# Entering the second feed-forward block: the last head pair's 1/z and the sums of squares on VectorE, three output tiles interleaved, statistics one tile later

## The chip, the cores and the metric

The kernel runs on one core of one Trainium2 chip. The metric is the device time of one execution in microseconds (us). Before the change three runs took 2205.42, 2205.99 and 2206.07 us; the median is 2205.99 us. The profile is one execution, taken with the hardware profiler.

The engines are named as the profile names them: PE multiplies matrices (PEld is its weight load), DVE is VectorE, ACT is ScalarE, POOL is GpSimd and SP is SyncE. SP, ACT and POOL also issue DMA transfers. Each engine executes its own instructions in the order in which the program wrote them, and waits at an instruction until its inputs are there.

## The reference, cut to what matters

A decoder trunk of two layers over 1024 positions of 1024 features. Layer 0 mixes tokens with a short gated convolution, layer 1 with dilated attention (16 heads of 64). A SwiGLU feed-forward block follows each.

```python
for i in range(DEPTH):                       # DEPTH = 2
    h = rms_norm(x, mix_norm[i])
    if i % N_MIXERS == 0:
        x = x + short_conv_mixer(h, ...)
    else:
        x = x + dilated_attention_mixer(h, ..., rel_bias)
    h = rms_norm(x, ffn_norm[i])
    x = x + swiglu(h, ffn_w_gate[i], ffn_w_up[i], ffn_w_down[i])
return rms_norm(x, final_norm)

def rms_norm(x, g):
    return x * rsqrt(mean(x * x, axis=-1) + EPS) * g
```

Two parts of it matter here. The attention output of a head is a sum `o` over keys divided by a sum of weights `z`; the kernel computes `o` and `z` and then multiplies `o` by 1/z. It is followed by the output projection with `attn_w_out`, which is added to x. Then `rms_norm` needs, for every position, the sum of squares over all 1024 features of the new x, before the feed-forward block can use any of it.

## The kernel before

The residual stream is held transposed, as eight tiles `X[0..7]` of 128 features by 1024 positions. Everything is 32-bit; a product takes three matmuls, because both operands are split into a rounded high part and a low remainder. `split` (L128) makes the two parts: ACT copies the high part (L138), DVE subtracts it from the source (L139). Weights come as raw slabs by SP's DMAs (`load_raw`, L148) and are split in the order of the list `ops`; `ensure` (L159) writes the splits up to a given place of that list into the program, and `take` hands one out and ensures one more ahead.

Attention works through eight pairs of heads. `slot` writes the instructions of one head and fills them up with matmuls of an independent product (`dense`). `finish` (L1482) turns the sums of a pair into attention output. For pairs 0 to 6 it sends z to DRAM, reads it back as a 128x16 tile, takes the reciprocal there, and reads 1/z back, spread over the partitions. For the last pair the first half of the positions is done on DVE directly, in two pieces of 256 columns (L1516, then o times 1/z, L1510, then the split into `o_hi` and `o_lo`). The second half goes through DRAM on POOL's queue (L1503, L1505, reciprocal of a 128x8 tile at L1528, L1529, L1530), and what remains to be done with it, the function `rest`, is put into the list `last_part`.

The output projection is done in two groups of heads. The first five pairs are multiplied beneath the attention. The last three pairs (k = 5, 6, 7, where 7 is the last pair) are `group1` of `into_ffn(1, ...)`, which calls `by_columns` (L1168): the first half of the positions (column half 0) for all eight output tiles n, then the second half. In column half 0 the first `AO_WIDE` = 5 tiles are interleaved on PE: k = 5 of all five, k = 6 of all five, then k = 7 of all five. The other tiles follow one by one, nine matmuls each. After each tile come, in this order: `add_to_x` (DVE, L459), `added` (which ensures the coming weight slabs), `each` (which is `chained`) and `between`.

`chained` (L411) squares the new half tile on ACT (L420) and sums the squares. Tile 0 is squared into `acc`, tile 1 into a second sum. Tiles 2 to 5 are added by accumulating DMAs that POOL issues (L422), alternately to the two. Tiles 6 and 7 and the second sum are added by DVE (L423).

`between` sends the half tile to DRAM from ACT's queue (L1211). At tile 3 of column half 0 it asks for the first feed-forward slabs (L1214) and runs `rest`. At tile 7 it finishes the sum and loads ACT's table for the square root (L1222). In column half 1, after tile 0, it writes the statistics of the first half: four small matmuls that sum over the partitions (L438), a square root (L441), a reciprocal (L442), a diagonal tile (L447), and three sums of raw weights (`combos`, L186). After tile 1 a matmul spreads the result (L454) and ACT copies it to `rstd` (L455). From there tiles 1 to 7 each carry one or two steps of `first_half` (L1061: DVE normalises a half tile, L1056, ACT and DVE split it, L518 and L519) and of `gained` (L1073: ACT writes the other half of the tile, times its gain, over the first half; for n > 3 POOL adds two of these with an accumulating DMA, L1082).

The feed-forward block follows in the same instruction streams: after its first product `last_step` writes the last split of `first_half` and the last addition of a square, after its second product come the statistics of the second half (L438 again), and after its third product the spread and `second_half` (L1084).

The first layer uses the same `into_ffn` with i = 0 and four interleaved tiles.

Of the kernel before, what the change touches and what calls it, by code (L numbers as in the profile page):

```python
# [10 lines left out]
F32 = mybir.dt.float32  # L11
F32R = mybir.dt.float32r
AF = mybir.ActivationFunctionType
ALU = mybir.AluOpType
# [3 lines left out]
S = 1024  # L18
# [5 lines left out]
HALF = 512  # L24
NPAIR = H // 2
# [20 lines left out]
AO_WIDE = 5  # L46
# [48 lines left out]
def trunk(ctx: ExitStack, tc: tile.TileContext, x, gains_in, cwi, ck, cwo, wqkv, wo, relb,  # L95
          wg, wu, wd, oneh, ident, out):
    nc = tc.nc
# [3 lines left out]
    dram = ctx.enter_context(tc.tile_pool(name="dram", bufs=1, space=DRAM))  # L101
# [5 lines left out]
    scope = {}  # L107

    def half_page(name, dt=F32):
        return scope["pool"].tile([128, 512], dt, name=name, tag="half", bufs=scope["halves"])  # L110
# [259 lines left out]
    X = [None] * KT  # L370

    class Norm:
        def __init__(self, gi):
            self.g = gi
            self.h = {}
            self.acc = self.rstd = None
            self.put_off = None

        def flush(self):

# [30 lines left out]
        def chained(self, k, c0, c1):  # L411

            s = slice(c0, c1)
            if self.acc is None:
                self.acc, self.rstd = page("acc"), page("rstd")
            acc = self.acc[:, s]
            if k == 1:
                self.odd = half_page("acc2")
            to = half_page("sq") if k > 1 else self.odd if k else acc
            nc.scalar.activation(to, X[k][:, s], AF.Square)  # L420
            if 1 < k < 6:
                nc.gpsimd.dma_start(out=(acc, self.odd)[k % 2], in_=to, accum_op=ALU.add)  # L422
            add = lambda t: nc.vector.tensor_tensor(out=acc, in0=acc, in1=t, op=ALU.add)  # L423
            if k == KT - 1:
                self.flush()
                add(self.odd)
                self.odd = None
            if k > 5:
                self.put_off = lambda: add(to)
# [759 lines left out]
    def into_ffn(i, norm):  # L1189

        sw = Swiglu(i, norm)

        pre = []
        first_op = [k for k, f in ops].index(("m", (i, 0), 1))

        def step(k):
            next(pre[0], None)
            sw.gained(k)

        def group1(key, ks, acts):  # L1200
            def added(j, n):

                if j == 0 and n > 3:
                    if n + 2 < KT:
                        ensure(op_state[1] + 1)
                    ensure(first_op + n - 4)
                elif j and n < 2:
                    ensure(first_op + n + 4)

            def between(j, n):  # L1210
                nc.scalar.dma_start(spill[n][:, half(j)], X[n][:, half(j)])  # L1211
                if j == 0:
                    if n == 3:
                        load_raw(raw_base[i] + 3)  # L1214
                        if not i:
                            nc.scalar.activation(less, gains, AF.Copy, scale=-1.0)
                        if last_part:
                            last_part.pop()()
                    elif n == KT - 1:
                        norm.flush()  # L1220
                        if i:
                            nc.scalar.activation(scratch, eps, AF.Sqrt)  # L1222
                elif n == 0:
                    pre.append(norm.stats(0, HALF))
                    next(pre[0])
                    for m in (6, 7):
                        combos[i, 0](m)
                else:
                    if n == 1:
                        run(pre.pop())  # L1230
                        pre.append(sw.first_half())
                    for k in ((0,), (1,), (2, 3), (4,), (5,), (6,), (7,))[n - 1]:
                        step(k)

            by_columns((key, 1), ks, acts, HALVES, lambda n, c: norm.chained(n, *c), between,
                       AO_WIDE if key == "ao" else 4, added=added)

        def last_step():
            run(pre[0])
            norm.flush()  # L1240

        return sw, group1, norm.stats(HALF, S), last_step


# [9 lines left out]

    vdram = [dram.tile([S, 256], F32, name=f"vdram{g}") for g in range(NPAIR // 2)]

    zdram = [[dram.tile([2, S], F32, name=f"{x}dram{n}") for x in "zr"] for n in range(NPAIR)]

    def blk(j):
        return (j // 4) * HALF + (j % 4) * 8  # L1260
# [1 line left out]
    def attention(norm):  # L1262
# [11 lines left out]
        parts = {}  # L1274
# [207 lines left out]
        def finish(p):  # L1482

            o, z = OZ.pop(p)
            if p < NPAIR - 1:
                zd, rd = zdram[p]
                nc.sync.dma_start(zd, z[0:65:64])
                yield
                zc = scope["pool"].tile([128, 16], F32, name="zc", tag="zc", bufs=2)
                nc.sync.dma_start(zc, bass.AP(zd.tensor, zd.offset, [[16, 128], [1, 16]]))  # L1490
                yield
                nc.vector.reciprocal(zc, zc)
                nc.sync.dma_start(bass.AP(rd.tensor, rd.offset, [[16, 128], [1, 16]]), zc)
                yield
                nc.sync.dma_start(z, bass.AP(rd.tensor, rd.offset, [[S, 2], [0, 64], [1, S]]))
                yield
                put_off.append((p, o, z))
                return

            zd, rd = zdram[p]  # L1500
            wide = lambda t: bass.AP(t.tensor, t.offset, [[HALF, 2], [1, HALF]])
            thin = lambda t: bass.AP(t.tensor, t.offset, [[8, 128], [1, 8]])
            nc.gpsimd.dma_start(wide(zd), z[0:65:64, HALF:])  # L1503
            zc = scope["pool"].tile([128, 8], F32, name="zl", tag="zl", bufs=1)
            nc.gpsimd.dma_start(zc, thin(zd))  # L1505
            acts[p] = page("o_hi", F32R), page("o_lo", F32R)

            def scaled(c0, c1):
                q = slice(c0, c1)
                nc.vector.tensor_tensor(out=o[:, q], in0=o[:, q], in1=z[:, q], op=ALU.mult)  # L1510

            def parts(h):
                split(o[:, half(h)], [t[:, half(h)] for t in acts[p]])

            for c in (0, 256):
                nc.vector.reciprocal(z[:, c:c + 256], z[:, c:c + 256])  # L1516
                scaled(c, c + 256)
                if c:
                    parts(0)
                yield  # L1520

            def rest():
                scaled(HALF, S)
                parts(1)

            last_part.append(rest)
            yield
            nc.vector.reciprocal(zc, zc)  # L1528
            nc.gpsimd.dma_start(thin(rd), zc)  # L1529
            nc.gpsimd.dma_start(z[:, HALF:], bass.AP(rd.tensor, rd.offset, [[HALF, 2], [0, 64], [1, HALF]]))  # L1530
            yield

        def attended():

# [157 lines left out]
    nc.vector.memset(eps, EPS)  # L1692
    nc.vector.memset(zcol, 0.0)

    last_part = []
    with tc.tile_pool(name="first", bufs=1) as scope["pool"]:
        scope["halves"] = 20
        conv = Conv(Norm(0))
# [2 lines left out]
        norm = Norm(1)  # L1701
# [11 lines left out]
    with tc.tile_pool(name="third", bufs=1) as scope["pool"]:  # L1713
# [3 lines left out]
        norm = Norm(4)  # L1717
# [135 lines left out]
```

## Time and profile before

| | |
|---|---|
| runs | 2205.42, 2205.99, 2206.07 us |
| span of the profiled execution | 2203.1 us; its own time is the span and about 2.9 us around it, taken from the median of the runs |
| PE busy | 2138.2 us, 97% of the span |
| DVE busy | 1752.9 us, 80% |
| ACT busy | 1000.5 us, 45% |
| POOL busy | 170.7 us, 8% |
| mean granted PE clock | 0.989 |

How to read it: the page lists busy time by engine for the whole span. A PE that is 97% busy says little about one stage, so the stage of the change is read from timelines of single engines (start, duration, line, operation, and in brackets the idle time before it and what ended it), from groups of instructions within a window, and from windows with the granted clock. The stage lies between 1484 and 1555 us.

### The profile page before, as it was taken

The numbers are of one execution on the slowest core, as the hardware profiler recorded it, in microseconds if no ns is written. First come the engines' busy times: TensorE is split into PE (matmuls) and PEld (weight loads), VectorE is DVE, ScalarE is ACT, GpSimd is POOL, SyncE is SP. The second block draws the span as 40 slices with busy tenths as digits, with TensorE's granted clock in tenths as the row PEclk, the third lists the DMA queues.
The fourth block names the chain that finished last, engine by engine and source line by source line (L and its number), as shares of the span: only waits on it lengthen the run. The fifth ranks groups of instructions, "written<-read, shape, count | busy, mean of one in ns | idle before, by whom it ended". The sixth has DMA issues, their size and how long they took to land. (4 is left out here: it accounts for less than half of the span.)

```text
span 2203.1 us, 30573 instructions
## 1 busy us (share of the span) xinstructions
PE 2138.2 (97%) x11138; PEld 1825.5 (83%) x11138; DVE 1752.9 (80%) x3229; ACT 1000.5 (45%) x1812; POOL 170.7 (8%) x224
## 2 busy tenths in 40 slices
PE   7899999999999999999999999998999999999998
PEld 6788888778888878878999998886778888888887
DVE  7797758988888798865677777866888888889886
ACT  6433426434444444445455455534544444454435
POOL 0000001100101000010111111112000101000000
PEclk9999999999999999999999999998999999999999
DMA  4122543223323384323333333446223233366432
GB/s 155 55 86 71 210 153 87 96 91 100 116 96 120 117 281 144 119 68 131 91 91 92 94 97 90 152 154 170 77 77 102 105 105 111 96 226 204 158 91 77
DMA packets 135345, 261.89 MB, mean 119 GB/s; under 512 B 48328, under 2 KB 59608, under 8 KB 135194
## 3 DMA queue, kind: packets, MB, share of 16 engines
q1 hardware_dynamic: 75978, 184.80, 26.3%
q0 software_dynamic: 18048, 52.03, 7.0%
q10 hardware_dynamic: 41168, 23.10, 3.5%
q8 instruction: 88, 1.44, 0.3%
q14 instruction: 63, 0.52, 0.1%
HBM read 187.31 MB, written 66.27 MB: 115 GB/s over the span
## 5 line engine op out<-in xcount | busy, mean ns | idle before, releaser
L526 PE MATMUL bank<-b,w 128*128 128x512 f32 x1784 | 704.6, 395 | 25.6 <-DVE part L536 6.4
L528 PE MATMUL bank<-b,w 128*128 128x512 f32 x1784 | 700.4, 393 | 8.9 <-DVE w L139 8.9
L527 PE MATMUL bank<-b,w 128*128 128x512 f32 x1784 | 701.4, 393 | 0.0
L526 PEld LDWEIGHTS bank<-b,w 128*128 128x128 f32 x1784 | 338.6, 190 | 102.6 <-ACT part L532 7.4
L528 PEld LDWEIGHTS bank<-b,w 128*128 128x128 f32 x1784 | 338.7, 190 | 84.2 <-DVE w L139 13.1
L527 PEld LDWEIGHTS bank<-b,w 128*128 128x128 f32 x1784 | 338.7, 190 | 69.2 <-issue 0.7
L138 ACT ACTIVATE w<-combo 128x512 fp32r<-128x512 f32 (+2 forms) x464 | 234.5, 534 | 281.5 <-DVE combo L186 275.5
L139 DVE TENSOR_TENSOR w<-combo,w 128x512 fp32r<-128x512 f32 (+2 forms) x464 | 260.9, 576 | 57.5 <-ACT w L138 55.2
L532 ACT ACTIVATE part<-bank 128x512 f32<-128x512 f32 x168 | 99.5, 593 | 269.7 <-PE bank L528 258.6
L139 DVE TENSOR_TENSOR w<-raw,w 128x512 fp32r<-128x512 f32 (+2 forms) x316 | 169.4, 561 | 15.6 <-ACT w L138 14.1
L536 DVE TENSOR_TENSOR part<-part,bank 128x256 f32<-128x256 f32 (+1 forms) x348 | 159.1, 488 | 26.4 <-PE bank L528 14.2
L138 ACT ACTIVATE w<-raw 128x512 fp32r<-128x512 f32 (+2 forms) x316 | 150.7, 519 | 46.0 <-PE bank L528 11.2
L747 DVE TENSOR_TENSOR x<-x,bank 128x512 f32<-128x512 f32 x168 | 114.6, 682 | 30.7 <-PE bank L528 30.7
L347 PE MATMUL bank<-w_hi,w 128*128 128x512 f32 (+1 forms) x320 | 121.3, 379 | 4.4 <-ACT w L138 4.4
L349 PE MATMUL bank<-w_hi,w 128*128 128x512 f32 (+1 forms) x320 | 119.3, 373 | 0.9 <-DVE w L139 0.9
L348 PE MATMUL bank<-w_lo,w 128*128 128x512 f32 (+1 forms) x320 | 119.0, 372 | 0.0
L459 DVE TENSOR_TENSOR x<-x,bank 128x512 f32<-128x512 f32 (+1 forms) x104 | 66.1, 643 | 65.6 <-PE bank L349 57.3
L186 DVE TENSOR_TENSOR combo<-raw 128x512 f32<-128x512 f32 (+1 forms) x160 | 103.2, 645 | 4.0 <-DMA raw<-in_conv_w_in 4.0
L347 PE MATMUL bank<-h_hi,w_hi 128*128 128x512 f32 x256 | 104.6, 408 | 0.0
L349 PE MATMUL bank<-h_hi,w_lo 128*128 128x512 f32 x256 | 100.2, 391 | 0.7 <-DVE w_lo L139 0.7
L348 PE MATMUL bank<-h_lo,w_hi 128*128 128x512 f32 x256 | 99.9, 390 | 0.0
L1130 ACT ACTIVATE part<-part 128x512 f32<-128x512 f32 x66 | 39.7, 628 | 107.5 <-DVE part L536 107.5
(252 smaller groups left out, 3842.7 us busy)
## 6 DMA issues: line engine op xcount, KB each, us to landing
hin<-part SPq DMA_DIRECT2D x126, 256.0 KB
raw<-in_ffn_w_gate SPq DMA_DIRECT2D x44, 512.0 KB
raw<-in_ffn_w_up SPq DMA_DIRECT2D x44, 512.0 KB
part<-sum POOLq DMA_DIRECT2D x72, 256.0 KB, 2.7
raw<-in_ffn_w_down SPq DMA_DIRECT2D x48, 384.0 KB
x<-spill SPq DMA_DIRECT2D x24, 512.0 KB
raw<-in_attn_w_qkv SPq DMA_DIRECT2D x24, 512.0 KB
raw<-in_conv_w_in SPq DMA_DIRECT2D x21, 512.0 KB
```

The source lines that it names most:

```text
L138: nc.scalar.activation(hi, src, AF.Copy)
L139: eng.tensor_tensor(out=lo, in0=src, in1=hi, op=ALU.subtract)
L186: eng.tensor_tensor(out=c, in0=a, in1=b, op=op)
L347: nc.tensor.matmul(b, whi[:, a], ahi[:, s], start=first, stop=False)
L348: nc.tensor.matmul(b, whi[:, a], alo[:, s], start=False, stop=False)
L349: nc.tensor.matmul(b, wlo[:, a], ahi[:, s], start=False, stop=last)
L526: nc.tensor.matmul(b, hi[:, a], bhi, start=start and k == 0, stop=False, skip_group_check=True)
L527: nc.tensor.matmul(b, hi[:, a], blo, start=False, stop=False, skip_group_check=True)
L528: nc.tensor.matmul(b, lo[:, a], bhi, start=False, stop=k == n - 1, skip_group_check=True)
L532: nc.scalar.activation(t, b, AF.Copy)
L536: nc.vector.tensor_tensor(out=t, in0=t, in1=b, op=ALU.add)
L747: nc.vector.tensor_tensor(out=X[n][:, half(h)], in0=X[n][:, half(h)], in1=b, op=ALU.add)
```

## The change

For i = 1 only, unless said otherwise:

1. `finish` of the last pair takes all four pieces of 256 columns on DVE. The four small DMAs, the 128x8 reciprocal, `rest` and `last_part` are gone, and so are the DRAM tiles for that pair.
2. `chained` no longer uses accumulating DMAs or the second sum when `by_dma` is false (it stays true for i = 0). Every square of tiles 1 to 7 is added to `acc` by DVE, one tile later than it is made.
3. Three tiles instead of five are interleaved in column half 0. `ahead_ao` in the attention keeps the constant 5, so the splits of weight slabs 0 to 4 stay where they were; the slabs 5 and 6, which `by_columns` ensured ahead of its first products, are now ensured with tile 4.
4. The statistics of column half 0 are written after tile 1 of column half 1, not after tile 0; the spread and the steps of `first_half` and `gained` start a tile later, with two steps at tile 2 and two at tile 7.

```diff
@@ class Norm
             self.put_off = None
+            self.by_dma = True
@@ chained
             acc = self.acc[:, s]
+            if not self.by_dma and k:
+                to = half_page("sq")
+                nc.scalar.activation(to, X[k][:, s], AF.Square)
+                self.flush()
+                self.put_off = lambda: nc.vector.tensor_tensor(out=acc, in0=acc, in1=to, op=ALU.add)
+                return
             if k == 1:
                 self.odd = half_page("acc2")
@@ into_ffn
         sw = Swiglu(i, norm)
+        norm.by_dma = not i
+        begin = i
@@ between
                         if not i:
                             nc.scalar.activation(less, gains, AF.Copy, scale=-1.0)
-                        if last_part:
-                            last_part.pop()()
                     elif n == KT - 1:
                         norm.flush()
                         if i:
                             nc.scalar.activation(scratch, eps, AF.Sqrt)
-                elif n == 0:
+                elif n == begin:
                     pre.append(norm.stats(0, HALF))
                     next(pre[0])
                     for m in (6, 7):
                         combos[i, 0](m)
-                else:
-                    if n == 1:
+                elif n > begin:
+                    if n == begin + 1:
                         run(pre.pop())
                         pre.append(sw.first_half())
-                    for k in ((0,), (1,), (2, 3), (4,), (5,), (6,), (7,))[n - 1]:
+                    plan = ((0, 1), (2,), (3,), (4,), (5,), (6, 7)) if i else ((0,), (1,), (2, 3), (4,), (5,), (6,), (7,))
+                    for k in plan[n - begin - 1]:
                         step(k)
 
             by_columns((key, 1), ks, acts, HALVES, lambda n, c: norm.chained(n, *c), between,
-                       AO_WIDE if key == "ao" else 4, added=added)
+                       3 if key == "ao" else 4, added=added)
@@ attention
-    zdram = [[dram.tile([2, S], F32, name=f"{x}dram{n}") for x in "zr"] for n in range(NPAIR)]
+    zdram = [[dram.tile([2, S], F32, name=f"{x}dram{n}") for x in "zr"] for n in range(NPAIR - 1)]
@@ finish
-            zd, rd = zdram[p]
-            wide = lambda t: bass.AP(t.tensor, t.offset, [[HALF, 2], [1, HALF]])
-            thin = lambda t: bass.AP(t.tensor, t.offset, [[8, 128], [1, 8]])
-            nc.gpsimd.dma_start(wide(zd), z[0:65:64, HALF:])
-            zc = scope["pool"].tile([128, 8], F32, name="zl", tag="zl", bufs=1)
-            nc.gpsimd.dma_start(zc, thin(zd))
             acts[p] = page("o_hi", F32R), page("o_lo", F32R)
@@ finish
-            for c in (0, 256):
+            for c in range(0, S, 256):
                 nc.vector.reciprocal(z[:, c:c + 256], z[:, c:c + 256])
                 scaled(c, c + 256)
-                if c:
-                    parts(0)
+                if c % HALF:
+                    parts(c // HALF)
                 yield
-
-            def rest():
-                scaled(HALF, S)
-                parts(1)
-
-            last_part.append(rest)
-            yield
-            nc.vector.reciprocal(zc, zc)
-            nc.gpsimd.dma_start(thin(rd), zc)
-            nc.gpsimd.dma_start(z[:, HALF:], bass.AP(rd.tensor, rd.offset, [[HALF, 2], [0, 64], [1, HALF]]))
-            yield
@@ trunk
-    last_part = []
```

## The prediction

> **What bounds the kernel now.** I first looked for PE's idle time around the entry to the second feed-forward block, in the timeline of PE (start, duration, line, operation, idle time before it and its releaser).
>
> ```profile
> span 2203.1 us, 30573 instructions
> ```
> ```profile
> 1490.47 0.39 PE L347 MATMUL bank<-w_hi,w 128*128 128x512 f32 x1
> ...
> 1504.52 0.39 PE L349 MATMUL bank<-o_hi,w 128*128 128x512 f32 x1
> 1508.26 0.80 PE L347 MATMUL bank<-w_hi,w 128*128 128x512 f32 x1 [3.35 <-ACT w L138]
> ...
> 1519.96 1.87 PE L438 MATMUL bank<-ones,acc 128*128 128x1 f32 x8 [4.17 <-DVE acc L423]
> ...
> 1547.51 1.05 PE L438 MATMUL bank<-ones,acc 128*128 128x1 f32 x8 [3.55 <-DVE acc L423]
> ```
>
> The group of the last three pairs starts at 1490.47. PE stops three times: for the weights of tile 7, and for each of the two statistics. The chain of work that ended last (start, duration, what) says what stands behind the three stops; its last row here serves a rival below.
>
> ```profile
> 1496.96 9.40 DMA z<-rdram
> ...
> 1511.74 6.58 DMA acc<-sq
> ...
> 1537.06 6.90 DMA acc<-sq
> ...
> 1976.59 5.75 DMA raw<-in_ffn_w_down
> ```
>
> All three are transfers that the change removes: 1/z coming back from DRAM (DVE stands in `rest` until it lands, and the split of tile 7's weights is queued behind it), and twice the last accumulating DMA. The windows (length, busy time and instructions of PE, PEld, DVE, ACT and POOL, granted clock, DMA share, GB/s) show a second price and the state of the next stage.
>
> ```profile
> 1508.26:1514.30 6.04, 5.88 (x13) 4.21 (x14) 5.68 (x10) 4.46 (x8) 1.68 (x2) 0.50 0.92 259
> ...
> 1547.51:1552.20 4.69, 4.69 (x18) 3.87 (x19) 4.43 (x8) 2.02 (x5) 0.37 (x1) 0.64 0.31 56
> 1552.20:1577.00 24.80, 24.80 (x109) 20.19 (x108) 22.36 (x37) 15.45 (x26) 0.00 (x0) 1.00 0.08 22
> ```
>
> After a stop PE's clock is at half for some microseconds. From 1552.2 it is whole again: 109 matmuls in 24.80 us, 0.2275 us each. PE and DVE are both nearly full from there, so whatever the statistics at 1547.51 gain is passed on by both.
>
> **Which engine decides once the transfers are gone.** PE's own work from 1490.47 to the second statistics is 16 half tiles of 9 matmuls, 24 matmuls of the first two feed-forward products and 2 of the spread, 170 x 0.2275 = 38.7 us, and 1.05 us for the first statistics: it could be there at 1530.2. DVE has more to do, and the change adds to it. So I keep an account of DVE from 1490.6 to 1547.5, 56.9 us. Its groups there (busy time, mean ns, then idle time before them and releasers):
>
> ```profile
> L459 DVE TENSOR_TENSOR x<-x,bank 128x512 f32<-128x512 f32 x18 | 12.2, 683 | 5.4 <-PE bank L349 5.3
> L1056 DVE SCALAR_TENSOR_TENSOR hcol<-x,gains,rstd 128x512 f32<-128x512 f32 x8 | 6.0, 746 | 0.6 <-ACT rstd L455 0.6
> ...
> L423 DVE TENSOR_TENSOR acc<-acc,sq 128x512 f32<-128x512 f32 x4 | 2.8, 688 | 1.9 <-DMA acc<-sq 1.8
> ...
> L139 DVE TENSOR_TENSOR o_lo<-o,o_hi 128x512 fp32r<-128x512 f32 x2 | 1.4, 692 | 1.5 <-ACT o_hi L138 1.5
> L423 DVE TENSOR_TENSOR acc<-acc,acc 128x512 f32<-128x512 f32 x2 | 1.4, 692 | 5.3 <-DMA acc<-sq 5.3
> ...
> L1510 DVE TENSOR_TENSOR o<-o,z 128x512 f32<-128x512 f32 x1 | 0.7, 691 | 5.5 <-DMA z<-rdram 5.5
> L1528 DVE RECIPROCAL zl<-zl 128x8 f32<-128x8 f32 x1 | 0.2, 204 | 0.9 <-DMA zl<-zdram 0.9
> L442 DVE RECIPROCAL r<-r 128x4 f32<-128x4 f32 x1 | 0.2, 178 | 1.1 <-ACT r L441 1.1
> ```
> ```profile
> 1484.87 1.75 DVE L1516 RECIPROCAL z<-z 128x256 f32<-128x256 f32 x1
> ...
> 1488.84 0.42 DVE L1510 TENSOR_TENSOR o<-o,z 128x256 f32<-128x256 f32 x1
> 1490.02 0.69 DVE L139 TENSOR_TENSOR o_lo<-o,o_hi 128x512 fp32r<-128x512 f32 x1 [0.76 <-ACT o_hi L138]
> ...
> 1492.97 0.98 DVE L139 TENSOR_TENSOR w<-raw,w 128x384 fp32r<-128x384 f32 x2
> ...
> 1533.54 0.68 DVE L459 TENSOR_TENSOR x<-x,bank 128x512 f32<-128x512 f32 x1
> 1534.14 0.74 DVE L1056 SCALAR_TENSOR_TENSOR hcol<-x,gains,rstd 128x512 f32<-128x512 f32 x1
> ```
>
> The idle times add up to 22.2 us; the 0.76 of the row at 1490.02 ended before the window, which leaves 21.4. A full-width operation takes 0.68, but the next starts after 0.60 (1533.54 to 1534.14), so each one that is followed by a wait costs 0.08 more. There are about twelve such now and I count four or five afterwards: 0.6 us back.
>
> **Part 1, 1/z by DVE.** Two reciprocals of 256 columns, 1.75 each, stand in the program at places where the last products of the first five pairs are added. Two multiplications of 0.42 take the place of one of 0.69, and the reciprocal of 0.20 goes: 3.5 + 0.15 - 0.2 = 3.45 us added. In DVE's order from 1490.63: add 0.60, reciprocal 1.75, product 0.42, add 0.60, reciprocal 1.75, product 0.42, the wait for ACT's `o_hi` 0.76 (as at 1490.02), `o_lo` 0.60. Tile 0 is therefore added at 1497.5, where the row of L459 now shows DVE idle for PE: its 4.2 us before tile 0 covered the reciprocals. Four small DMAs leave POOL's queue; nothing else in it was late.
>
> **Part 2, squares by DVE.** Before, DVE made 3 of the additions of a half, 6 in all (the two L423 groups); now 7 and 7. That is 8 x 0.60 = 4.8 us. ACT's squares stay, and the eight accumulating transfers go. Their cover is gone with them: where DVE waited for a DMA it now works, so these 4.8 us are on the path, and cheaper than the waits of 1.9 and 5.3.
>
> **Parts 3 and 4, the order.** No work is added. Tiles 0 to 2 need `o_hi` at 1490.47 + 18 x 0.2275 = 1494.6, and its first half is there by 1490.7. But slabs 5 and 6, split at 1492.97 while PE was busy, now come with tile 4, behind the square of tile 3 on ACT. The rows of ACT (same window):
>
> ```profile
> L420 ACT ACTIVATE sq<-x 128x512 f32<-128x512 f32 x12 | 7.5, 629 | 1.8 <-DVE x L459 1.5
> ...
> L1222 ACT ACT_TABLE_LOAD x1 | 1.3, 1283 | 0.0
> ...
> L138 ACT ACTIVATE w<-raw 128x384 fp32r<-128x384 f32 x2 | 1.0, 507 | 0.0
> ...
> L455 ACT ACTIVATE rstd<-bank 128x512 f32<-128x512 f32 x1 | 0.6, 580 | 0.0
> ```
>
> Tile 3 is added from about 1500.0 (tiles 0, 1, 2 and one square after 1497.5). Its square starts at 1500.7 and takes 0.63; the high part of slab 5 takes 0.51, so its low part can start at 1501.9. DVE is free at 1501.2: it waits 0.7. PE is through with tile 4 at 1490.47 + 45 x 0.2275 = 1500.7 and stands for about 1.5 us in all.
>
> The statistics a tile later find the additions of column half 0 done: tile 7 should be added near 1509 and its square near 1511, while PE ends tile 1 of the second half near 1512. So the stop of 4.17 vanishes rather than moves. The steps of `first_half` start a tile later, and this makes DVE, not PE, late at the second statistics.
>
> **Waits that stay on DVE:** 0.76 for `o_hi`; 0.7 for slab 5; at the spread, x of tile 2, then its square 0.63 and the copy 0.58 on ACT, with nothing for DVE to do: 1.3; after the table load of 1.28 behind the last square of column half 0, some 0.4; small ones 0.2. Together 3.4 us. None of these places had a price of its own before, so I bound the sum from 1.5 (only the first two) to 5.
>
> **The sum.** 21.4 idle + 0.6 - 3.45 - 4.8 - 3.4 = 10.3 us. DVE's last addition and with it the second statistics come 10.3 us earlier, near 1537.2. PE is there 4 to 5 us before. What follows is unchanged in work and order, so I carry the 10.3 to the end: span 2203.1 - 10.3 = 2192.8. The median of the runs, 2205.99, lies 2.9 above the span, so the forecast is 2195.7.
>
> The stop of 4 to 5 us that remains will again be followed by slow matmuls like those from 1547.51 (clock 0.64); this keeps that price and does not enter the sum. The Trainium skill, "TensorE: Matmul & The Clock Gate", Part 1: The HAM clock gate, says that PE's clock falls to half after an idle window of about 3.4 us and returns after as long at work. The trace agrees at 1508.26: idle 3.35, then clock 0.50 for 6.04 us. By this rule the new stop of 1.5 us for slab 5 costs no clock, and the time would be the forecast.
>
> **Rivals.**
>
> *The clock falls at slab 5 too.* Two shorter stops elsewhere in the trace, with the clock after them:
>
> ```profile
> 1603.79 0.50 PE L528 MATMUL bank<-b,w 128*128 128x512 f32 x1 [1.94 <-DVE w L139]
> ...
> 1650.80 0.68 PE L526 MATMUL bank<-b,w 128*128 128x512 f32 x1 [2.22 <-ACT part L532]
> ```
> ```profile
> 1650.80:1654.46 3.66, 3.66 (x9) 2.88 (x10) 2.38 (x7) 1.78 (x6) 0.00 (x0) 0.53 0.00 0
> 1603.79:1607.00 3.21, 3.21 (x14) 2.68 (x15) 3.17 (x7) 1.09 (x3) 0.00 (x0) 1.00 0.02 5
> ```
>
> 1.94 us left the clock whole, 2.22 halved it. With a stop nearer 2.2, tiles 5 to 7 run at half speed. At 1508.26 this cost half of 6.04, 3.0 us, and DVE would then wait for PE. Gain 7.3, time 2198.7.
>
> *PE decides.* If DVE fits its work into fewer waits, the bound is PE's 1530.2 and the 1.5 of slab 5: 1531.7, which is 15.8 before 1547.5. Time 2190.2. Against it: DVE would have to lose all 3.4 of waits and 2 us of work.
>
> *Given back, or not done.* The stage after it could wait for something that did not move, weights above all. For it: that stage was nearly full. Against it: from 1552.20 the DMA share is 0.08 and both engines work on data that comes earlier too. Time 2206.
>
> *Slower: slabs late behind the spills.* The raw slab of tile 7 and the first feed-forward slabs are now asked for at tile 3, behind four DMAs that send x to DRAM, and one slab in the trace did wait for such a transfer:
>
> ```profile
> 1482.70 0.38 SPq L152 DMA_DIRECT2D raw<-in_attn_w_out  x1
> ...
> 1488.13 0.38 SPq L152 DMA_DIRECT2D raw<-in_ffn_w_gate  x1
> 1506.62 3.45 SPq L152 DMA_DIRECT2D raw<-in_ffn_w_up  x2
> ```
> ```profile
> SPq L152 <- DMA spill<-x: 20.8, 2, 18.0
> ```
>
> If slab 7, now issued at 1482.70, waited until 1506.6 as that one did, and the first feed-forward slab came behind it, with some 6 us of transfer (5.75 at 1976.59) and 1.5 for the first of the two, it would land at 1514. Its split on ACT stands before the square of tile 4, due near 1502.8. From a landing after 1513 all of the gain is eaten; at 1514 and a slow clock after so long a stop the time is about 2208. Against it: the slab at 1488.13 was asked for at this same place, behind the same four spills, and was issued ten microseconds before the first of them ran.
>
> **How the numbers follow.** Forecast 0.55, clock at slab 5 0.18, PE decides 0.10, given back 0.10, slower 0.07. The bounds of the waits (1.5 to 5) move the forecast by -1.9 to +1.6. The range 2190.0 to 2200.5 takes in the first three cases. A difference under 0.2%, 4.4 us, can hardly be told from none in this kernel; the first three cases lie beyond it. So faster 0.83, within 0.2% 0.10, slower 0.07.
>
> **What would show it.** Right: no `z<-rdram` after 1490 and no `acc<-sq` transfer there; first statistics without a stop; tile 0 added at about 1497.5; a stop of 1 to 2 us before tile 5; the second statistics near 1537, released by DVE's addition of a square, with PE idle 4 to 5 us before; from there every row early by the same amount. Wrong: DVE idle for more than 5 us in the stage, a granted clock of half after tile 5, slabs that land after 1502, or a stage behind it that no longer keeps its distance.

## The result, and the profile after

| | before | changed |
|---|---|---|
| median of four runs, us | 2206.03 | 2196.84 |
| lowest to highest | 2205.42 to 2206.45 | 2194.63 to 2197.13 |
| span of the profiled execution | 2203.1 | 2192.6 |
| mean granted PE clock in it | 0.989 | 0.992 |

The ratio is 0.9953, with a 95% interval of 0.9941 to 0.9964: 9.2 us faster in the medians, 10.5 us in the two profiled executions. The changed kernel's profiled execution took 2194.63 us, 2.0 us more than its span; the other three took 2196.66 to 2197.13 us at a clock of 0.991.

PE's timeline of the changed kernel shows the three places where PE used to stop.

```profile
1502.57 0.50 PE L347 MATMUL bank<-w_hi,w 128*128 128x512 f32 x1 [1.58 <-ACT w L138]
...
1513.03 0.94 PE L445 MATMUL bank<-ones,acc 128*128 128x1 f32 x8
...
1537.16 1.05 PE L445 MATMUL bank<-ones,acc 128*128 128x1 f32 x8 [4.02 <-DVE acc L422]
```

The stop of 3.35 us before tile 7 is gone, and one of 1.58 before tile 5 has come (PE waits for the split of weight slab 5). The first statistics have no stop. The second come at 1537.16 instead of 1547.51, after 4.02 us of waiting that DVE's last addition of a square ends, not a transfer.

DVE's groups in the window from 1490.6 to 1537.5 (busy time, mean ns, idle time before them and its releasers) answer the account in the prediction.

```profile
L466 DVE TENSOR_TENSOR x<-x,bank 128x512 f32<-128x512 f32 x18 | 12.1, 679 | 0.0
L422 DVE TENSOR_TENSOR acc<-acc,sq 128x512 f32<-128x512 f32 x14 | 9.6, 685 | 0.3
L1063 DVE SCALAR_TENSOR_TENSOR hcol<-x,gains,rstd 128x512 f32<-128x512 f32 x8 | 5.9, 747 | 1.2 <-ACT rstd L462 1.2
L139 DVE TENSOR_TENSOR w<-raw,w 128x512 fp32r<-128x512 f32 (+1 forms) x9 | 5.6, 640 | 0.6 <-ACT w L138 0.5
...
L1518 DVE RECIPROCAL z<-z 128x256 f32<-128x256 f32 x2 | 3.5, 1745 | 0.0
...
L139 DVE TENSOR_TENSOR o_lo<-o,o_hi 128x512 fp32r<-128x512 f32 x2 | 1.4, 692 | 1.5 <-ACT o_hi L138 1.5
```

The 5.4 us in which DVE waited for PE before adding to x are gone: the reciprocals fill them. Left are 0.5 for slab 5, 1.2 at the spread, and 1.5 for the two `o_hi`, of which 0.76 straddles the window's start. With the small ones it is 3.0 us.

**One measure for all runs.** The entry begins at times that differ by up to 4.4 us between executions (the first reciprocal at 1484.67 to 1489.07), so spans mix what happens before the stage with the stage. I measure the stage from DVE's first reciprocal of the last pair to DVE's first operation that uses the statistics of the second half. Before, the first row is at 1484.87 (in the prediction), and the timeline of DVE ends the stage with:

```profile
1554.54 2.50 DVE L1086 TENSOR_TENSOR x<-x,rstd 128x512 f32<-128x512 f32 x4 [2.54 <-ACT rstd L455]
```

In the changed kernel the two rows are:

```profile
1485.52 1.74 DVE L1518 RECIPROCAL z<-z 128x256 f32<-128x256 f32 x1
...
1544.19 2.50 DVE L1093 TENSOR_TENSOR x<-x,rstd 128x512 f32<-128x512 f32 x4 [2.54 <-ACT rstd L462]
```

That is 69.7 us before and 58.7 us after: 11.0 less. From the end of the stage to the end of the span it is 648.6 and 648.4.

One run below, of the kernel with four additions less in half 1, took 9714.16 us; nothing on record says why, and its ratio leaves it out, though its median does not.

### The profile page after: what moved, and what is told of

The parts are those of the page before. It is cut to its first block, busy times and chain, and to the rows that moved or that the text cites. A ratio compares the mean times of both kernels' runs of the same rounds, so it can differ in the third digit from the quotient of the medians.

```text
span 2192.6 us, 30554 instructions
## 1 busy us (share of the span) xinstructions
PE 2133.3 (97%) x11138; PEld 1821.9 (83%) x11138; DVE 1759.4 (80%) x3239; ACT 999.8 (46%) x1812; POOL 161.9 (7%) x212
## 4 chain that ended last, share of the span: by engine, by line
PE 78%; DVE 13%; ACT 4%; DMA 3%; issue 2%; ACTq 0%; SPq 0%; DVEq 0%
PE bank L533 15%; PE bank L535 15%; PE bank L534 15%; PE bank L349 5%; PE bank L347 5%; PE bank L348 5%; PE bank L1463 4%; PE bank L625 3%; PE bank L627 3%; PE bank L628 3%; DVE w L139 2%; DVE b L526 1%; DVE combo L186 1%; PE bank L1391 1%; PE bank L1390 1%
## 5 line engine op out<-in xcount | busy, mean ns | idle before, releaser
L534 PEld LDWEIGHTS bank<-b,w 128*128 128x128 f32 x1784 | 338.5, 190 | 69.7 <-issue 0.7
```

Of the source, the lines that this page charges most:

```text
L534: nc.tensor.matmul(b, hi[:, a], blo, start=False, stop=False, skip_group_check=True)
```

## The experiments

My theory: with the transfers gone DVE's work decides this stage, and what the stage gains is passed on whole. Rivals: PE's stops decide; a single part carries all; the clock falls at slab 5; the gain is given back behind the stage. The runs came in three groups, each with its own runs of the kernel before on the same chip. In the table, stage and rest (from the stage's end to the end of the span) are worked out from the one profiled execution of each kernel, by the rows named above.

| kernel | median us | before beside it | ratio, 95% interval | stage us | rest us |
|---|---|---|---|---|---|
| before | | | | 69.7 | 648.6 |
| changed | 2196.84 | 2206.03 | 0.9953 [0.9941, 0.9964] | 58.7 | 648.4 |
| part 1 alone | 2204.71 | 2208.00 | 0.9985 [0.9976, 0.9994] | 67.8 | 648.2 |
| part 2 alone | 2202.40 | 2208.00 | 0.9976 [0.9967, 0.9984] | 65.0 | 648.9 |
| parts 1 and 2 | 2195.09 | 2207.89 | 0.9940 [0.9926, 0.9953] | 61.8 | 649.6 |
| five tiles interleaved | 2193.89 | 2208.00 | 0.9939 [0.9927, 0.9952] | 58.2 | 648.1 |
| slabs 5, 6 early | 2195.35 | 2207.89 | 0.9948 [0.9936, 0.9960] | 57.2 | 648.0 |
| statistics at old place | 2197.12 | 2208.00 | 0.9950 [0.9938, 0.9963] | 59.4 | 650.1 |
| four additions less, half 1 | 2195.80 | 2207.41 | 0.9941 [0.9927, 0.9955] | 57.7 | 648.5 |
| four additions less, half 0 | 2199.55 | 2207.41 | 0.9959 [0.9947, 0.9972] | 58.6 | 648.5 |
| last square early | 2195.63 | 2207.41 | 0.9949 [0.9936, 0.9963] | 58.2 | 649.8 |
| last square early, five tiles | 2193.60 | 2207.89 | 0.9940 [0.9928, 0.9951] | 56.4 | 649.6 |
| additions on POOL | 2198.04 | 2207.41 | 0.9964 [0.9952, 0.9977] | 63.3 | 648.4 |
| changed, again | 2197.40 | 2207.89 | 0.9955 [0.9942, 0.9968] | 59.4 | 648.4 |

### Part 1 alone

To the kernel before, the edit of `finish` alone:

```diff
-            nc.gpsimd.dma_start(wide(zd), z[0:65:64, HALF:])
...
-            for c in (0, 256):
+            for c in range(0, S, 256):
...
```

> The kernel before with part 1 alone: all four pieces of 1/z on DVE; squares still by accumulating DMAs, five tiles interleaved, statistics at their old place. My account: the stop of 3.35 us before tile 7 goes, and tile 5 is squared near 1504 instead of 1510.8. The accumulating DMAs then run one after the other, and the first statistics still wait for the last one, near 1514 instead of 1520. Gain 5 to 6 us, time near 2200.5. A rival: the first transfer chain hides whatever tile 7 gains, then the first statistics stay near 1520 and the time within 1.5 us of before. Another rival: part 1 is the whole change, and the time is that of the changed kernel, near 2196.

PE's timeline and POOL's, of this kernel:

```profile
1521.10 1.87 PE L438 MATMUL bank<-ones,acc 128*128 128x1 f32 x8 [9.57 <-DVE acc L423]
```
```profile
1504.70 1.77 POOL L422 DMA_DIRECT2D acc<-sq  x2 [28.95 <-DMA spill<-x]
1512.43 0.84 POOL L422 DMA_DIRECT2D acc<-sq  x1 [5.96 <-ACT scratch L1222]
1516.26 0.84 POOL L422 DMA_DIRECT2D acc<-sq  x1 [2.98 <-issue]
```

The stop before tile 7 is gone, and the time with it went into one stop of 9.57 us at the first statistics. The accumulating DMAs begin no sooner than 1504.7 (the row names a transfer of x to DRAM as what ended last), and the fourth is issued at 1516.3. From the first reciprocal (1488.25 here) the first statistics come after 32.9 us, before after 35.1: 2.2 us earlier, not the 5 to 6 I expected. The rival by which the chain of transfers hides the gain is nearer. The median falls by 3.3 us.

### Part 2 alone

To the kernel before, the edit of `chained` alone:

```diff
+            if not self.by_dma and k:
...
+        norm.by_dma = not i
```

> The kernel before with part 2 alone: squares added by DVE, 1/z of the second half still through DRAM, five tiles interleaved, statistics at their old place. My account: the stop before tile 7 stays (3.3 us, until 1508), DVE then has fourteen operations of 0.60 between tile 4 and the last square of column half 0, so the first statistics come near 1516.8 instead of 1520, and the second near 1542 instead of 1547.5. Gain 5 to 6 us, time near 2200.5. If it and part 1 alone add up to the whole (10.5 in the profiles), the parts are in series, each taking away transfers at another place. The rival, that DVE's 4.8 us of additions eat what the transfers gave, says no change, 2205 to 2207.

PE's timeline of this kernel:

```profile
1508.46 0.50 PE L347 MATMUL bank<-w_hi,w 128*128 128x512 f32 x1 [3.40 <-ACT w L138]
...
1517.24 1.05 PE L445 MATMUL bank<-ones,acc 128*128 128x1 f32 x8 [1.86 <-DVE acc L422]
...
1541.72 1.87 PE L445 MATMUL bank<-ones,acc 128*128 128x1 f32 x8 [2.67 <-DVE acc L422]
```

The expected places were 1516.8 and 1542, and the median fell by 5.6 us (expected 5 to 6): DVE's additions are cheaper than the transfers even with the way of 1/z through DRAM left in. In the profiles the two parts do not add up to the whole, 1.9 + 4.7 = 6.6 of 11.0; the medians give 3.3 + 5.6 = 8.9 of 9.2, and show no such gap.

### Five tiles interleaved again

To the changed kernel:

```diff
-                       3 if key == "ao" else 4, added=added)
+                       AO_WIDE if key == "ao" else 4, added=added)
```

> The changed kernel with five tiles interleaved again, which also puts the splits of slabs 5 and 6 back before the group's first products. PE's stop of 1.6 us before tile 5 should go. If DVE decides, the time does not follow PE: the same work in another order, less DVE's 0.5 us of waiting for slab 5, so the time is between 1 us below and 0.5 us above that of the changed kernel, and PE's stop before the second statistics grows from 4.0 to 5 us or more. If PE's stops decide, the time falls by 1.6 us.

PE's timeline of this kernel:

```profile
1510.95 1.05 PE L445 MATMUL bank<-ones,acc 128*128 128x1 f32 x8
...
1515.19 1.13 PE L461 MATMUL bank<-diag,ones 128*128 128x512 f32 x2 [0.99 <-DVE diag L454]
...
1536.02 1.05 PE L445 MATMUL bank<-ones,acc 128*128 128x1 f32 x8 [4.03 <-DVE acc L422]
```

The stop before tile 5 is gone. Counted from the first reciprocal, PE reaches the first statistics 1.5 us sooner, then waits 0.99 for DVE's diagonal tile, and the second statistics are only 0.5 us sooner. So PE's stop of 1.58 was worth 0.5, as much as DVE had waited for slab 5: DVE decides at the spread and after it. The stop before the second statistics did not grow as I had expected, because a part of it moved to the spread. The median lies 14.1 us below before, the changed kernel's 9.2; the intervals (0.9927 to 0.9952, 0.9941 to 0.9964) overlap, so that more than the 0.5 was gained is not shown.

### Statistics at the old place

To the changed kernel:

```diff
-        begin = i
+        begin = 0
-                    plan = ((0, 1), ...) if i else ((0,), ...)
+                    plan = ((0,), (1,), (2, 3), (4,), (5,), (6,), (7,))
```

> The changed kernel with the statistics and the steps of the first half back at their old place, a tile earlier. If DVE decides, PE has a stop of about 1.3 us again at the first statistics, which DVE's last addition of column half 0 releases, and the time stays within 1 us of the changed kernel, because DVE's work is the same. If the later place is what removed the stop of 4.2 us, the time is 3 us or more longer.

PE's timeline of this kernel:

```profile
1503.02 0.76 PE L347 MATMUL bank<-w_hi,w 128*128 128x512 f32 x1 [2.15 <-ACT w L138]
...
1513.82 1.05 PE L445 MATMUL bank<-ones,acc 128*128 128x1 f32 x8 [0.74 <-DVE acc L422]
...
1538.28 1.05 PE L445 MATMUL bank<-ones,acc 128*128 128x1 f32 x8 [2.66 <-DVE acc L422]
```

The first statistics wait 0.74 us; the stage is 0.7 us longer, and the clock was at 0.51 behind the stop before tile 5 in this execution. The ratio agrees with the changed kernel's. The stop of 4.17 did not vanish because the statistics moved, but because the transfers went.

### Four additions less in column half 1, and in column half 0

To the changed kernel, here for half 1; for half 0 the condition has `c0 == 0`. Both leave the squares of tiles 2 to 5 of that half out of the sum:

```diff
-                self.put_off = lambda: nc.vector.tensor_tensor(...)
+                if not (1 < k < 6 and c0 == HALF):
+                    self.put_off = lambda: nc.vector.tensor_tensor(...)
```

> The changed kernel without the additions of the squares of tiles 2 to 5 in column half 1: that part of the sum is left out. Four DVE operations of 0.60 less between the first and the second statistics. If DVE decides, the second statistics come 2.4 us earlier and the time falls by 2.4 us. If the spread's chain through ACT or PE itself decides, it falls by less than 0.5 us.

> The changed kernel without the additions of the squares of tiles 2 to 5 in column half 0: that part of the sum is left out. If DVE decides from tile 0 on, the time falls by up to 2.4 us too. But the first two of these additions stand before the split of slab 5, for which DVE waits for ACT anyway, and after tile 7 DVE waits for the table load, so some of it turns into waiting: I expect 1.2 to 2.0 us. If PE decides in this half, nothing moves, since PE's work is the same.

PE's timeline without the additions in half 1, and then without those in half 0:

```profile
1504.84 0.50 PE L347 MATMUL bank<-w_hi,w 128*128 128x512 f32 x1 [2.79 <-ACT w L138]
...
1538.41 1.05 PE L446 MATMUL bank<-ones,acc 128*128 128x1 f32 x8 [1.62 <-DVE acc L423]
```
```profile
1514.47 0.95 PE L446 MATMUL bank<-ones,acc 128*128 128x1 f32 x8
...
1538.46 1.05 PE L446 MATMUL bank<-ones,acc 128*128 128x1 f32 x8 [4.04 <-DVE acc L423]
```

Half 1: from the first statistics (1516.83 here) to the second it takes 21.6 us, in the changed kernel 24.1 (1513.03 to 1537.16). That is 2.5 less for four additions, 0.63 each, as expected: in this stretch DVE decides. The whole stage shortened by only 1.0, because in this execution the stop before tile 5 was 2.79 us and the clock stood at 0.56 for the 3.8 us after it; the first statistics came 1.5 us later, counted from the first reciprocal. That is the rival of the fallen clock, seen: PE left the stop 17.05 us after the first reciprocal, exactly as in the changed kernel, so the 1.5 us are the clock's alone.

Half 0: nothing. The first statistics come 27.6 us after the first reciprocal, in the changed kernel 27.5. From slab 5 to the first statistics PE runs through without a stop, and DVE had room. My expectation of 1.2 to 2.0 us was wrong: in column half 0 DVE decides only up to slab 5.

### The last square early

To the changed kernel:

```diff
                     for k in plan[n - begin - 1]:
+                        if i and k == KT - 1:
+                            norm.flush()
                         step(k)
```

> The changed kernel with the last addition of a square put before DVE's work on tile 7 instead of behind it: the same instructions in another order. The second statistics should come about 2 us earlier, near 1535.1, and PE's stop before them should shrink from 4.0 to 2 us. If only DVE's total decided, the time would stay. I expect that the chain from the statistics to the spread, in which DVE stands idle 2.5 us, starts earlier and runs beneath DVE's remaining work: 1 to 2.5 us faster than the changed kernel, the larger figure if the shorter stop leaves PE's clock whole.

PE's timeline of this kernel, then a window (its columns as in the prediction):

```profile
1501.95 0.50 PE L347 MATMUL bank<-w_hi,w 128*128 128x512 f32 x1 [1.93 <-ACT w L138]
...
1534.49 1.83 PE L445 MATMUL bank<-ones,acc 128*128 128x1 f32 x8 [1.97 <-DVE acc L422]
```
```profile
1534.49:1541.40 6.91, 6.91 (x20) 5.80 (x21) 6.38 (x11) 3.94 (x9) 1.68 (x2) 0.51 0.52 95
```

The second statistics come 2.1 us earlier and the stop is halved, as expected. But the clock was low at once, and stayed so for 6.9 us, from the statistics to the spread; in the changed kernel this stretch takes 5.3. So 0.5 us is left of the 2.1.

### Additions on POOL

To the changed kernel:

```diff
+                eng = nc.gpsimd if k < 6 else nc.vector
-                self.put_off = lambda: nc.vector.tensor_tensor(...)
+                self.put_off = lambda: eng.tensor_tensor(...)
```

> The changed kernel with the squares of tiles 1 to 5 added by POOL, which is idle there, and only tiles 6 and 7 by DVE. If DVE's count of operations is all that matters, ten operations of 0.60 less bring the second statistics up to 5 us earlier, as far as PE lets them. The Trainium skill, SBUF - State Buffer, on the shared port pair, says that a POOL operation and a DVE operation with two SBUF inputs lock each other out for the whole instruction; by it DVE's operations would be held up as long as POOL's last, and with POOL slower than DVE the kernel would lose. I expect no gain: 0 to 5 us slower than the changed kernel.

Groups of this kernel, POOL's (from 1498 to 1545) and DVE's (from 1491 to 1544):

```profile
L423 POOL TENSOR_TENSOR acc<-acc,sq 128x512 f32<-128x512 f32 x10 | 13.5, 1349 | 47.3 <-ACT sq L420 47.2
```
```profile
L467 DVE TENSOR_TENSOR x<-x,bank 128x512 f32<-128x512 f32 x18 | 12.0, 680 | 2.3 <-PE bank L349 2.3
L139 DVE TENSOR_TENSOR w<-raw,w 128x512 fp32r<-128x512 f32 (+1 forms) x9 | 8.1, 919 | 1.2 <-ACT w L138 1.1
L1064 DVE SCALAR_TENSOR_TENSOR hcol<-x,gains,rstd 128x512 f32<-128x512 f32 x8 | 7.0, 888 | 1.2 <-ACT rstd L463 1.2
```

An addition takes 1349 ns on POOL against 685 on DVE, and DVE's operations with two operands in SBUF grow meanwhile (640 to 919 ns, 747 to 888), while the addition to x, which reads one operand from PSUM, stays at 680. The Trainium skill, "SBUF — State Buffer", Who interferes with whom, says that only the port pair which POOL and DVE share makes them wait for each other; the trace agrees. The stage is 4.6 us longer in the profile, but 2.6 of that came before the first statistics, where the clock stood at 0.50 for 6.5 us after a stop of 2.97 before tile 5; how much is POOL's is not shown. In the medians no difference from the changed kernel can be told (0.9964 and 0.9953, intervals overlapping).

### The changed kernel again, slabs early, parts 1 and 2, and both edits together

Slabs early, to the changed kernel:

```diff
-        ahead_ao = [k for k, f in ops].index(("ao", 1, AO_WIDE - 1))
+        ahead_ao = [k for k, f in ops].index(("ao", 1, AO_WIDE + 1))
```

Parts 1 and 2 is the changed kernel with the two edits of "five tiles interleaved" and "statistics at the old place". The last kernel has the edits of "five tiles interleaved" and "the last square early".

> The changed kernel once more, unchanged, beside the next three on the same chip. Two executions of the runs before stood before tile 5 for 2.15 and 2.79 us and had the clock at half after it; in the first profile of the changed kernel the stop was 1.58 and the clock stayed whole. If the length of that stop varies between executions with where PE stands when DVE takes the first reciprocal, this kernel's times spread over some 3 us, and its profile has from the first of the last pair's reciprocals to DVE's first operation on the second half's statistics either 58.7 us (clock whole) or about 60 (clock fallen).

> The changed kernel with only the splits of slabs 5 and 6 put back ahead of the group; three tiles stay interleaved. The stop before tile 5 goes, so the clock cannot fall there. If the interleave itself matters, this differs from the run with five tiles interleaved; I expect it to agree with that one within 1 us: 58.2 us from the first reciprocal to the second half's statistics in use, and a median 1 to 3 us below the changed kernel's beside it.

> Parts 1 and 2 together without parts 3 and 4: five tiles interleaved, statistics at their old place. Alone they shortened the stage by 1.9 and 4.7 us in their profiles, 6.6 in sum; the whole change by 11.0. If the rest comes from parts 3 and 4, this kernel gains about 6.6 and stays some 4 us behind the changed kernel. If each part alone only uncovers the transfers of the other, it gains 10.5 to 12 and is level with the changed kernel or up to 2 us before it.

> The changed kernel with five tiles interleaved and the last addition of a square ahead of DVE's work on tile 7. The stop before the second statistics was 1.97 us with the second edit alone, and its gain of 2.1 us there fell to 0.5 because the clock was low for longer behind it. With both I expect 57.7 us over the stage, 0.5 us below five tiles interleaved alone, and a time equal to that within what can be measured; 1.5 us better if the clock stays whole after the shorter stop.

PE's timelines, first of the changed kernel again, then of parts 1 and 2, then of both edits together:

```profile
1501.72 0.50 PE L347 MATMUL bank<-w_hi,w 128*128 128x512 f32 x1 [1.05 <-ACT w L138]
...
1536.32 1.87 PE L445 MATMUL bank<-ones,acc 128*128 128x1 f32 x8 [4.02 <-DVE acc L422]
```
```profile
1512.04 1.76 PE L445 MATMUL bank<-ones,acc 128*128 128x1 f32 x8 [1.93 <-DVE acc L422]
...
1539.12 1.56 PE L445 MATMUL bank<-ones,acc 128*128 128x1 f32 x8 [2.04 <-DVE acc L422]
```
```profile
1515.11 1.05 PE L445 MATMUL bank<-ones,acc 128*128 128x1 f32 x8 [1.10 <-DVE acc L422]
...
1538.12 1.05 PE L445 MATMUL bank<-ones,acc 128*128 128x1 f32 x8 [1.67 <-DVE acc L422]
```

The changed kernel again: 2194.43 to 2202.83 us in six runs, an even wider spread than expected, with mean clocks of 0.992 to 0.989. Its stop before tile 5 was 1.05, in other executions with the same head of the stage 1.10 to 2.79. The end of that stop is DVE's: it lies 17.05 or 17.06 us after the first reciprocal in all six of them. Its length is what PE leaves over: PE began the group 3.90 (stop 2.79) to 5.64 us (stop 1.05) after that reciprocal, and the two add up to 6.68 to 6.70 each time. So the expectation about the length holds. The second statistics came 51.65 us after the first reciprocal, in the first profile 51.64. The stage took 59.4 us although the clock stayed whole at tile 5: here the second statistics themselves ran at half clock (1.87 us). The longer runs have the lower mean clocks, so the clock has a share in the spread; how large, and that tile 5 makes most of it, is not shown.

Slabs early: the stop is gone and the stage is 57.2 us, 1.0 below five tiles interleaved. That is not the interleave: DVE's two splits of slabs 5 and 6, at 1497.56 with five tiles (1.02 us for both), run here before the first reciprocal and so outside the measure; of the 1.5 us below the changed kernel, too, 1.0 are this. The median is 2.1 us below the changed kernel's beside it, as expected, with overlapping intervals.

Parts 1 and 2: the median is 12.8 us below before, so parts 3 and 4 are not needed for the gain; in sum the two alone had given 8.9, which the intervals do not separate from it. In its profiled execution, the slowest of its six, the stage gained only 7.9, with the clock low after stops of 1.93 and 2.04. Its six runs reach from 2190.38 to 2199.21. The run is thus clear in its times and unclear in its profile.

Both edits together: the shortest stage, 56.4 us, 13.3 below before, and the lowest median, 2193.60 us. The stop of 1.67 left the clock whole through the statistics; about 2.2 us after their start it fell to half for some 3 us. From the statistics to the spread the mean is thus near the changed kernel's, not at 0.51 as with the last square early alone (first this kernel, then the changed one):

```profile
1538.12:1543.50 5.38, 5.22 (x20) 3.79 (x20) 5.22 (x10) 3.94 (x9) 1.68 (x2) 0.71 0.49 89
```
```profile
1537.16:1542.50 5.34, 5.34 (x20) 4.39 (x21) 4.42 (x8) 2.02 (x5) 0.84 (x1) 0.68 0.48 87
```

Beside the changed kernel on the same chip (2197.40) it is 3.8 us faster in the medians; the intervals, 0.9928 to 0.9951 and 0.9942 to 0.9968, overlap. It is ahead of the kernel before beyond doubt, ahead of the changed one probably, and not to be told from five tiles interleaved (0.9939) or parts 1 and 2 (0.9940) by its ratio of 0.9940.

## Why the prediction was right, point by point

**What bounds the kernel: right.** The three transfers were what PE's stops waited for. Removing one kind alone gave 1.9 and 4.7 of the 11.0 us in the profiles, because the other still stopped PE (9.57 us in one stop with part 1 alone, 3.40 still before tile 7 with part 2 alone).

**Which engine decides: right for the sum, wrong for half of the stage.** I let DVE decide from 1490 to the second statistics. The runs show three stretches: DVE up to slab 5 (tile 5 begins 17.05 us after the first reciprocal, wherever PE stands); PE from slab 5 to the first statistics (four additions less in half 0: no change); DVE from there to the second (four less in half 1: 2.5 us), and there its order counts as well as its sum (last square early: 2.1 us). The sum came out because DVE's account and PE's were level there: in the changed kernel DVE's last addition of half 0 ended at 1512.05, and PE reached the statistics at 1513.03. My working showed PE the later of the two there (1512 against 1511), but did not draw this from it; that a sum over DVE alone came out is in part luck.

**Part 1: right.** 3.45 us of work came in, and tile 0 was added 12.6 us after the first reciprocal (1498.17), as forecast (1497.5 after 1484.87). The idle 5.4 us before the additions to x are 0.0 now.

**Part 2: right.** 0.685 us each, the next one after 0.60; 0.63 in the experiment. **Parts 3 and 4: right** that they add no work (with part 3 or part 4 undone the stage is 58.2 or 59.4 us, against 58.7), and that the stop for slab 5 is about 1.5 us (1.58, though 1.05 in the second profile). The stop at the first statistics did go.

**Waits that stay: 3.4 forecast, 3.0 measured.** The one at the spread was 1.2 (1.3), slab 5 0.5 (0.7), `o_hi` 0.76 (0.76).

**The sum.** 10.3 forecast; the second statistics came 10.35 us earlier, at 1537.16 (1537.2), the stage is 11.0 shorter, the span 10.5. The two differ because the changed execution entered the stage 0.65 us later. So the agreement to 0.1 us is luck: counted from the first reciprocal, the second statistics came 11.0 us earlier (51.64 after 62.64), 0.7 more than forecast, of which 0.4 are the waits. The price behind the last stop was kept, as assumed: from the statistics to the spread 5.3 us before and after (6.0 in the second profile of the changed kernel). PE's side of the stage shows what the 11.0 consist of: for the same matmuls (230 and 228 records) it was busy 58.4 us before, at a mean clock of 0.88, and 52.9 after, at 0.97. Half of the gain are stops that are gone, half are matmuls that no longer run at half clock.

**Carried to the end: right.** In all the profiled executions the time from the end of the stage to the end of the span is 648.0 to 650.1 us, 648.6 before. Nothing was given back, within 1.5 us.

**The rivals.** The clock falling at slab 5 is real: it was seen after stops of 2.15, 2.79 and 2.97 us in three other kernels with three tiles interleaved, at a price of 1.5 us in one, half of what I had put. It did not happen in either profile of the changed kernel. "PE decides" did not happen for the stage as a whole, and "given back" not at all. Slower did not either: SP issued the slabs asked for behind the spills long before those ran (ACT issued the first at 1498.89).

```profile
1483.16 0.33 SPq L152 DMA_DIRECT2D raw<-in_attn_w_out  x1
...
1486.55 0.33 SPq L152 DMA_DIRECT2D raw<-in_ffn_w_gate  x1
```

**Where it missed by 1.1 us.** The span was forecast as 2192.8 and is 2192.6; the median is 2196.84, not 2195.7. I had added the 2.9 us between one profile and the median of other runs; for the changed kernel the profiled execution was the quickest of four, and the same difference is 4.2.

## What to carry to other kernels

When several transfers feed one engine in turn, count what the engine would have to do if all were gone, and check the account for each stretch between two meetings of the engines; the sum can be right while a stretch belongs to another engine. Removing the first of two waits that lie close together can show little until the second is removed too, so parts tried alone can understate a change, as in the profiles here. Compare stages from a row that starts them to a row that ends them: here the executions entered the stage up to 4.4 us apart, as much as a part was worth.

## What the runs showed of the hardware that was not expected

PE's clock fell after shorter stops than I had reckoned with, and not at a fixed length. Where matmuls of 512 columns followed, before tiles 5 and 7, it stayed whole after 1.05, 1.10, 1.58 and 1.93 us, and was at half within half a microsecond after 2.15, 2.79, 2.97 and 3.35; after 3.40 (part 2 alone) it stayed whole for 1.9 us more and fell then. Where the statistics followed, eight small matmuls, it was low within half a microsecond after 1.93, 1.97, 2.04 and 2.67, and fell 1.0 to 2.4 us behind the end of stops of 1.10, 1.62, 1.67 and 2.66; 1.86 left it whole. The rule that I cited in the prediction, from the Trainium skill, "TensorE: Matmul & The Clock Gate", Part 1: The HAM clock gate, gives an idle window of about 3.4 us; these runs show a fall at once after 1.93, and one behind a stop of 1.10. Nor did the clock return after as long at work in the kernel before: from 1508.26 it was low for 6.04 us.

A shorter stop can cost as much as a longer one: after 4.02 us the changed kernel's statistics ran in 1.05 and the stretch to the spread took 5.3, while after 1.97 they ran in 1.83 and it took 6.9. The same stop does not cost the same either: after 4.02 us in its second profile the statistics ran in 1.87 and the stretch took 6.0. And one kernel on one chip spread over 8 us (2194.43 to 2202.83) with mean clocks from 0.992 to 0.989.
